# A two-layer hybrid attention block: maxima in steps of two banks, values in fewer and longer visits, and two gate tiles computed earlier

## The chip, the core and the metric

The program runs on one core of a Trainium2 chip. The metric is device time in microseconds, from launch to end. The engines are TensorE (PE, with its weight loads as PEld), VectorE (DVE), ScalarE (ACT), GpSimd (POOL) and SyncE (SP), which here issues DMAs alone. Matmul results land in PSUM, in banks of 512 fp32 columns.

## The reference

A two-layer block for 1024 latent tokens and 256 context tokens of width 1024. In each layer every token is normalised and modulated, projected to 2816 columns, mixed by three groups of heads, multiplied by a SiLU gate, and projected back with a residual. The change touches the first group, attention of all latent tokens to all 1280 tokens:

```python
shift, scale, gate = jnp.split(silu(c) @ w_mod[l] + b_mod[l], 3, axis=-1)
h = rms_norm(x, norm_gain[l]) * (1 + scale[:, None]) + shift[:, None]
aq, ak, av, ag, bz, bg, nq, nk, nv, ng = jnp.split(h @ w_in[l], SPLIT_POINTS, axis=-1)
...
kk = jnp.concatenate([k, k_ctx], axis=1)
vv = jnp.concatenate([v, v_ctx], axis=1)
s = jnp.einsum("bqkgd,bskd->bkgqs", q, k).astype(jnp.float32)
p = jax.nn.softmax(s, axis=-1)
o = jnp.einsum("bkgqs,bskd->bqkgd", p, v)
...
y = jnp.concatenate([a_out * silu(ag), b_out * silu(bg), n_out * silu(ng)], axis=-1) @ w_out[l]
x = x + gate[:, None] * y
```

There are eight query heads of 64 columns in two groups, each with its own key and value head.

## The kernel before, in words

**Stages.** Per layer: the modulation vector and the normalised, modulated, transposed activations, each split in a high and a low part (`hh`, `hl`); the input projections, as three matmuls for a product (high × high, low × high, high × low); neighbourhood attention (and, in layer 0, the context tokens' attention) in 28 units in layer 0 and 16 in layer 1; global attention in eight units; the output projection. In layer 0 the modulation runs in a loop over eight blocks of weights, `mod_rows`, `mod_set` and `first_h`, and the four features of `W` (the pooling projection) for the first 512 tokens are multiplied in the same loop, three blocks behind. The gate products of the attention heads, `gate_feat`, come late in the projection stage: four feature tiles by two halves of the tokens, of 24 matmuls each, stored to DRAM as `agd`.

**A unit of global attention** (`ga_unit`) is a pair of heads and 512 queries. Scores are computed with keys on the partitions, so that the maximum of a query lies across partitions. The maxima are therefore computed apart, with queries on the partitions, from the high parts only: `shift`, twenty steps for a unit, each a 512-column matmul into a single bank (or two of 256 columns), and a DVE reduction. `shift_rows` takes the result through a transpose into an extra row of the second query operand, so that `scores` come out with the maximum subtracted. Scores go by fifths of the keys (`kp` 0 to 4), two heads each: two key tiles into a pair of banks, one exponential of 1024 columns on ACT (L1032), and a running sum over keys on POOL (L1037, L1040), at `kp` 4 on DVE (L1040) with a fold (L1042). `values` multiplies the exponentials by the values into the bank `ps_c` (L1049). `finish` sums over partitions with a matmul by ones (L1058), takes the reciprocal through Ln and Exp on ACT (L1062, L1063) with a Newton step on DVE (L1065, L1066), multiplies by gate and output (POOL L1067, DVE L1068), and `store_u` writes high and low part (ACT L815, DVE L816).

**PSUM.** Three single banks `ps_b` are handed out in turn by `ps_one`, for maxima among others; `ps_c` is the accumulator; four banks `ps_w` serve as single banks in projections and as two pairs in attention, for scores.

**What sets the order.** PE's order is the order of the program text. The other engines' order is set by a scheduler that goes by dependencies, and a tile that is handed out again waits for its readers. Each engine works through its instructions in order, so one that waits holds all behind it. The steps of maxima form one list, `shifts`, of all eight units. `shift_step(n)` takes the next n. Some are taken during neighbourhood attention (`n_ahead`, 29 single-bank steps), and in global attention they are laid between scores and values, four or five for each `kp`. Within one `kp` the order is: scores of head 0, a step, values of the `kp` before for both heads, a step (two at `kp` 4), scores of head 1, two steps. `finish` of the unit before stands at the end of `kp` 2. `early(k, fn)` runs a load at neighbourhood unit k: the keys `gk(0)` and the first queries `gunits[i][4]`.

Of the kernel before, what the change touches and what calls it, by code (L numbers as in the profile page):

```python
# [31 lines left out]
GA_AHEAD = 8  # L32
# [42 lines left out]
def hybrid_block_kernel(  # L75
# [48 lines left out]

    def ps_one(name):
        wide.b += 1
        return ps_b[wide.b % 3]
# [177 lines left out]
    x0 = load_x(0, 4, [rows3(pm.tile([P, D], F32, name="xt", bufs=8)) for _ in range(4)])  # L305
# [25 lines left out]
    def mod_set(j, m):  # L331
        ps = ps_one("ps_sel")
# [7 lines left out]
    blocks = [mod_load(0)]  # L340
    ps = ps_one("ps_v")
# [32 lines left out]
    for l in range(DEPTH):  # L374
# [66 lines left out]


# [65 lines left out]
        else:  # L508
            W = []

            banks = [ps_bank("ps_feat") for _ in range(4)]
            rows = None
            x1 = [rows3(pm.tile([P, D], F32, name="xt", bufs=8)) for _ in range(4)]
            for j in range(KT + 4):
                if j < KT:
                    W.append(load_w_tile([(C_BZ, 512)], j))
                    if j + 1 < KT:
                        blocks.append(mod_load(j + 1))
                    if 2 <= j < 6:
                        load_x(2 + j, 1, x1[j - 2:j - 1])  # L520
                    nxt = mod_rows(blocks[j])
# [3 lines left out]
                if j == 4:  # L525
                    add1, done1 = h_norm(4)
                if 4 <= j < 8:
                    add1(x1[j - 4])
                if j == 7:
                    todo += h_steps(0, 4, done1(), wp, "sig")  # L530
                if j == KT:
# [5 lines left out]
                if j > KT:  # L537
                    fill(2)
                if 3 <= j < KT + 3:
                    for f in range(4):  # L540
                        feat_step(banks[f], W, j - 3, f, 0, 512)
            stx.close()
# [18 lines left out]
        fill(2)  # L561
        for f in range(2, 4):
            pool_in(f, 0, 512, banks[f])
        for t0, n in chunks[1:2]:
# [162 lines left out]
        def gate_out(ps, f, t0, n, s=None):  # L727
            g = s or wp.tile([P, 512], F32, name="gate", bufs=2)
            silu_to(g, ps, 512, s)
            SP.dma_start(out=agd[f, :, t0:t0 + n], in_=g)  # L730

# [4 lines left out]
        gates += [lambda f=f, t0=t0, n=n: gate_feat(f, t0, n) for f in range(4) for t0, n in chunks[:2]]  # L736
# [174 lines left out]
        for pr in range(2):  # L911
# [13 lines left out]
            else:  # L925
                early(s0 + 4, lambda: gk(0))
# [48 lines left out]
        def ga_unit(cc, g, pr):  # L975
# [16 lines left out]
            def shift(i):  # L992

                hi, j = divmod(i, 10)
                if i == 0:
                    load2()
                    st.mx = small.tile([P, 2, 4, 3], F32, tag="gmx", name="gmx")
                q1, mx = st.q1[hi], st.mx[:, hi]
                k1 = gk(g)[0]
                S = ps_one("ps_m")  # L1000
                if j < 8:
                    qt, half = divmod(j, 2)
                    PE.matmul(S, q1[:, qt * P:(qt + 1) * P], k1[:, half * 512:(half + 1) * 512], start=True, stop=True)  # L1003
                    DVE.reduce_max(out=mx[:, qt, half:half + 1], in_=S, axis=AX.X)  # L1004
                    return
                q0 = 2 * (j - 8)
                for i in range(2):
                    PE.matmul(S[:, i * 256:(i + 1) * 256], q1[:, (q0 + i) * P:(q0 + i + 1) * P], k1[:, SEQ:NT], start=True, stop=True)
                DVE.reduce_max(out=mx[:, q0:q0 + 2, 2], in_=S.rearrange("p (a b) -> p a b", a=2), axis=AX.X)
                if hi and j == 9:  # L1010
                    st.nn = small.tile([P, 8], F32, tag="gnn", name="gnn")
                    DVE.tensor_reduce(out=st.nn, in_=st.mx.rearrange("p h q k -> p (h q) k"), op=ALU.max, axis=AX.X, negate=True)
# [11 lines left out]
            def scores(hi, kp):  # L1024
                k1, k2 = gk(g)
                S = ps_pair("ps_st").rearrange("p (a b) -> p a b", a=2)
                for i in range(2):
                    kc = slice((2 * kp + i) * P, (2 * kp + i + 1) * P)
                    PE.matmul(S[:, i, :], k1[:, kc], st.q1[hi], start=True, stop=False)  # L1029
# [306 lines left out]
```

## Time and profile before

| | us |
|---|---|
| median of three runs | 1539.0 |
| the runs | 1536.47 to 1542.13 |
| profiled execution, its own time | 1539.72 |
| its span, first to last instruction | 1537.9 |
| PE busy | 1474.2 |
| DVE busy | 860.2 |
| ACT busy | 637.6 |
| POOL busy | 513.1 |
| layer 0: modulation | 0 to 65 |
| layer 0: neighbourhood and context attention | 391 to 513.3 |
| layer 0: global attention | 513.3 to 730.3 |
| layer 1: neighbourhood attention | 1126.8 to 1226.8 |
| layer 1: global attention | 1226.8 to 1442 |

A row of the timeline gives start, length, engine, line, and, in brackets, how long the engine stood idle before it and what released it. A group gives busy time, mean length of one instruction in ns, and the idle time before them. Line numbers are those of the kernel before. Matmuls overlap, so the time of one is read from start to start. In the orders shown below, lines are those of the kernel that is named.

### The profile page before, as it was taken

Reading aid. Unit: us, or ns where it says so; the run is one execution under the profiler, and the core shown is the slowest. Engines: PE = TensorE matmul, PEld = TensorE weight load, DVE = VectorE, ACT = ScalarE, POOL = GpSimd, SP = SyncE. Lnnn points to the kernel's source line nnn. Section 1 sums busy time; section 2 is a strip of 40 time slices with the busy share of each in tenths; the row PEclk is TensorE's granted clock in tenths of the full one; section 3 lists DMA queues with packets and bytes.
Section 4 is the critical chain, followed back from the end, with each engine's and each line's share of the span. In section 5 each row is a group of like instructions: output and inputs, shape, how many; then the busy total and the mean of one; then the engine's idle time right before and its main releaser. Section 6 shows DMA issues by size and latency. Waiting matters only on the chain.

```text
span 1537.9 us, 22259 instructions
## 1 busy us (share of the span) xinstructions
PE 1474.2 (96%) x8001; PEld 1072.8 (70%) x8001; DVE 860.2 (56%) x1666; ACT 637.6 (41%) x1220; POOL 513.1 (33%) x630
## 2 busy tenths in 40 slices
PE   5999999999999999998999999999998999999999
PEld 3787777788888555553788888878787854544577
DVE  3645234552678678875533543464358868786522
ACT  4543132333676444444312452332466544444400
POOL 0232336000134556565001233460013265565300
PEclk9999999999999999999999999999999999999999
DMA  9436455537745200101413222243697301001331
GB/s 317 140 97 219 133 158 162 165 107 192 178 113 159 73 27 25 39 8 55 168 58 109 76 93 91 85 142 82 155 227 172 89 21 42 21 24 39 133 121 55
DMA packets 153039, 167.91 MB, mean 109 GB/s; under 512 B 35384, under 2 KB 112032, under 8 KB 152864
## 3 DMA queue, kind: packets, MB, share of 16 engines
q1 hardware_dynamic: 152928, 166.48, 37.0%
q8 instruction: 63, 1.03, 0.3%
q14 instruction: 48, 0.39, 0.1%
HBM read 126.45 MB, written 40.86 MB: 109 GB/s over the span
## 4 chain that ended last, share of the span: by engine, by line
PE 80%; DVE 8%; ACT 4%; DMA 3%; issue 3%; SPq 1%; POOL 0%; DVEq 0%; POOLq 0%; ACTq 0%
PE ps_w L418 8%; PE ps_w L419 8%; PE ps_w L420 8%; PE ps_c L1049 8%; PE ps_w L1204 4%; PE ps_w L1207 4%; PE ps_w L1205 4%; PE ps_w L1029 4%; PE ps_b L1003 4%; PE ps_w L1030 3%; PE ps_c L894 3%; PE ps_b L882 2%; PE ps_w L426 2%; PE ps_w L428 2%; PE ps_w L427 2%
## 5 line engine op out<-in xcount | busy, mean ns | idle before, releaser
L1032 ACT ACTIVATE gp<-ps_w 128x1024 f32<-128x1024 f32 x160 | 162.4, 1022 | 190.9 <-PE ps_w L1030 155.3
L418 PE MATMUL ps_w<-wh,hh 128*128 128x512 f32 (+1 forms) x624 | 235.7, 378 | 2.2 <-ACT wh L287 2.2
L419 PE MATMUL ps_w<-wl,hh 128*128 128x512 f32 (+1 forms) x624 | 229.0, 367 | 1.0 <-DVE wl L288 1.0
L420 PE MATMUL ps_w<-wh,hl 128*128 128x512 f32 (+1 forms) x624 | 228.4, 366 | 0.0
L1004 DVE TENSOR_REDUCE gmx<-ps_b 128x1 f32<-128x512 f32 x256 | 171.7, 685 | 73.2 <-PE ps_b L1003 69.0
L1049 PE MATMUL ps_c<-gp,av 128*64 128x512 f32 x640 | 165.0, 609 | 10.3 <-ACT gp L1032 10.3
L1040 POOL TENSOR_TENSOR gacc<-gacc,gp 128x1024 f32<-128x1024 f32 x64 | 161.4, 2548 | 25.8 <-ACT gp L1032 25.5
L418 PEld LDWEIGHTS ps_w<-wh,hh 128*128 128x128 f32 x624 | 118.4, 190 | 27.8 <-issue 4.0
L419 PEld LDWEIGHTS ps_w<-wl,hh 128*128 128x128 f32 x624 | 117.8, 189 | 21.3 <-DVE wl L288 2.2
L420 PEld LDWEIGHTS ps_w<-wh,hl 128*128 128x128 f32 x624 | 117.6, 188 | 21.3
L1030 PE MATMUL ps_w<-gq,kst 128*128 128x512 f32 x320 | 126.7, 396 | 0.0
L1204 PE MATMUL ps_w<-woh,hh 128*128 128x512 f32 x272 | 109.5, 403 | 0.0
L1205 PE MATMUL ps_w<-wol,hh 128*128 128x512 f32 x272 | 107.4, 395 | 0.0
L639 DVE TENSOR_REDUCE qss<-sq 128x8 f32<-128x512 f32 (+2 forms) x58 | 31.1, 537 | 135.7 <-ACT sq L637 135.7
L1049 PEld LDWEIGHTS ps_c<-gp,av 128*64 128x64 f32 x640 | 42.5, 136 | 87.3 <-issue 65.2
L1037 POOL TENSOR_TENSOR gacc<-gp 128x1024 f32<-128x1024 f32 x32 | 75.8, 2369 | 50.0 <-ACT gp L1032 50.0
L288 DVE TENSOR_TENSOR wl<-wraw,wh 128x512 fp32r<-128x512 f32 (+1 forms) x96 | 66.3, 707 | 38.8 <-ACT wh L287 37.4
L1207 PE MATMUL ps_w<-woh,hl 128*128 128x512 f32 x272 | 85.6, 395 | 0.0
L426 PE MATMUL ps_w<-hh,wh 128*128 128x512 f32 (+1 forms) x208 | 81.6, 392 | 2.4 <-ACT wh L287 2.4
L866 ACT ACTIVATE prob<-ps_w,m 128x768 f32<-128x768 f32 (+2 forms) x88 | 72.7, 826 | 19.4 <-DVE m L853 7.4
L428 PE MATMUL ps_w<-hh,wl 128*128 128x512 f32 (+1 forms) x208 | 79.6, 382 | 0.0
L427 PE MATMUL ps_w<-hl,wh 128*128 128x512 f32 (+1 forms) x208 | 79.2, 381 | 0.0
(225 smaller groups left out, 2916.2 us busy)
## 6 DMA issues: line engine op xcount, KB each, us to landing
wmod<-in_w_mod_dram SPq DMA_DIRECT2D x48, 512.0 KB
wraw<-in_w_in_dram SPq DMA_DIRECT2D x64, 256.0 KB
gq<-qad SPq DMA_DIRECT2D x64, 128.0 KB
woraw<-in_w_out_dram SPq DMA_DIRECT2D x14, 512.0 KB
wraw<-in_w_in_dram SPq DMA_DIRECT2D x48, 128.0 KB
kst<-knd SPq DMA_DIRECT2D x16, 320.0 KB
qad<-qkhi SPq DMA_DIRECT2D x18, 256.0 KB
qad<-qklo SPq DMA_DIRECT2D x18, 256.0 KB
```

The source lines that it names most:

```text
L418: PE.matmul(ps[:, :n], a, wh[:, off:off + n], start=(k == 0), stop=False)
L419: PE.matmul(ps[:, :n], a, wl[:, off:off + n], start=False, stop=False)
L420: PE.matmul(ps[:, :n], b, wh[:, off:off + n], start=False, stop=(k == KT - 1))
L426: PE.matmul(ps[:, :n], wh[:, fs], hh[:, k, ts_], start=(k == 0), stop=False)
L1004: DVE.reduce_max(out=mx[:, qt, half:half + 1], in_=S, axis=AX.X)
L1030: PE.matmul(S[:, i, :], k2[:, kc], st.q2[hi], start=False, stop=True)
L1032: ACT.activation(out=p, in_=S, func=AF.Exp)
L1040: eng.tensor_tensor(out=st.acc[hi], in0=st.acc[hi], in1=pf, op=ALU.add)
L1049: PE.matmul(st.o[hi * 64:(hi + 1) * 64, :], av[:, kt, g * 64:(g + 1) * 64], st.p[hi, kp][:, i, :], start=(kt == 0), stop=(kt == NTT - 1))
L1204: PE.matmul(ps[:, i2, :], a, oh[:, cs], start=(k == 0), stop=False)
L1205: PE.matmul(ps[:, i2, :], a, ol[:, cs], start=False, stop=False)
L1207: PE.matmul(ps[:, i2, :], b, oh[:, i2 * 512:(i2 + 1) * 512], start=False, stop=(k == KT - 1))
```

## The change

**Maxima.** Steps of the first unit and of the first head of the second stay as they were. All others are made by `shift2`: five steps a head, each in a pair of banks, with one reduction of 1024 columns; the fifth holds the context keys of all four query tiles. The list has 103 steps instead of 168. 31 of them are taken in neighbourhood attention, one after each of a unit's two heads, in the last 16 units, and the loads of first keys and queries move with them.

**Scores** go to single banks, with one exponential of 512 columns for each. **Values** are taken at `kp` 2 and `kp` 4 for two fifths at a time; the last fifth of a unit comes at `kp` 1 of the next, with its sums and `finish`. `sums` copies them out of PSUM on ACT. In `finish` POOL takes both products with the gate, ACT the high part from POOL's result, DVE the low part. Running sums have buffers of their own (`accs`).

**Gates.** In layer 0, two of the four feature tiles for the first 512 tokens are multiplied in the modulation loop, into two of the `ps_b` banks, with eight loads of 128 KB added; they leave the later gate stage. Vector loads come ahead of the first tokens, and each later token tile is read one block later.

```diff
-GA_AHEAD = 8
+GA_AHEAD = 31
...
+                    G.append((hh[:, j, 512:768], hh[:, j, 768:1024]))
+                    raw = wp.tile([P, 512], F32, name="wraw", bufs=4)
+                    SP.dma_start(out=raw[:, 0:256], in_=w_in[l, j * P:(j + 1) * P, C_AG:C_AG + 256])
+                    split_w(G[j], raw[:, 0:256], slice(0, 256))
...
+                    for f in range(2):
+                        feat_step(ps_b[1 + f], G, j - 3, f, 0, 512)
...
-        gates += [lambda f=f, t0=t0, n=n: gate_feat(f, t0, n) for f in range(4) for t0, n in chunks[:2]]
+        gates += [lambda f=f, t0=t0, n=n: gate_feat(f, t0, n) for f in range(4) for t0, n in chunks[:2]
+                  if l or f > 1 or t0]
...
+            def shift2(hi, j):
+                if j == 0:
+                    (load2 if hi else shift_new)()
+                S = ps_pair("ps_m")
+                if j < 4:
+                    for half in range(2):
+                        shift_mm(hi, S, j, half * 512, half * 512, 512)
+                    DVE.reduce_max(out=st.mx[:, hi, j, 0:1], in_=S, axis=AX.X)
+                    return
+                for qt in range(4):
+                    shift_mm(hi, S, qt, qt * 256, SEQ, 256)
+                DVE.reduce_max(out=st.mx[:, hi, :, 1], in_=S.rearrange("p (a b) -> p a b", a=4), axis=AX.X)
+                shift_head(hi, 2)
...
-                S = ps_pair("ps_st").rearrange("p (a b) -> p a b", a=2)
+                p = ap_.tile([P, 2, 512], F32, name="gp", tag="prob", bufs=PB)
                 for i in range(2):
+                    S = ps_one("ps_st")
...
+                    ACT.activation(out=p[:, i, :], in_=S, func=AF.Exp)
...
+            def sums():
+                S = ps_one("ps_gs")
+                for hi in range(2):
+                    PE.matmul(S[hi * 64:(hi + 1) * 64, :], ones, st.acc[hi][:, 0:512], start=True, stop=True)
+                st.r0, st.t1 = [ap_.tile([P, 512], F32, name=nm, tag="fin", bufs=4) for nm in ("gr0", "gt1")]
+                ACT.activation(out=st.r0, in_=S, func=AF.Ln)
+                ACT.activation(out=st.t1, in_=S, func=AF.Copy)
...
                 POOL.tensor_tensor(out=gt, in0=gt, in1=st.osb, op=ALU.mult)
-                DVE.scalar_tensor_tensor(out=t1, in0=t1, scalar=-1.0, in1=gt, op0=ALU.mult, op1=ALU.mult)
-                store_u(f, cc * 512, 512, t1)
+                POOL.tensor_tensor(out=gt, in0=gt, in1=t1, op=ALU.mult)
+                hi, lo = hh[:, f, cs], hl[:, f, cs]
+                ACT.activation(out=hi, in_=gt, func=AF.Identity, scale=-1.0)
+                DVE.scalar_tensor_tensor(out=lo, in0=gt, scalar=-1.0, in1=hi.bitcast(F32), op0=ALU.mult, op1=ALU.subtract)
...
+        n_shifts = min(len(units), (GA_AHEAD + 1) // 2)
         for i in range(2):
-            early(len(units) - 12, gunits[i][4])
+            early(len(units) - n_shifts - 1, gunits[i][4])
+        early(len(units) - n_shifts, lambda: gk(0))
...
-                if lagv:
-                    lagv(0)
-                    lagv(1)
-                shift_step(2 if kp == 4 else 1)
+                if kp == 1 and pv:
+                    pv[2](4, 0)
+                    pv[2](4, 1)
+                    pv[7]()
+                    pv[3]()
+                elif kp in (2, 4):
+                    for j in range(4):
+                        values(kp - 2 + j // 2, j % 2)
                 scores(1, kp)
-                shift_step(2)
-                if kp == 2 and pv:
-                    pv[3]()
+                shift_step(2 if kp == 0 else 1)
```

ACT, in a middle unit of global attention of the kernel before, around the tail of the previous unit: `gr` is the reciprocal, `hh` the high part of the output, `gp` the exponentials.

```order
L1062 ACTIVATE gr_6166<-ps_b_71 128x512
L1063 ACTIVATE gr_6166<-gr_6166 128x512
L1032 ACTIVATE gp<-ps_w_3845 128x1024
L1032 ACTIVATE gp<-ps_w_3846 128x1024
L815 ACTIVATE hh<-gt_6169 128x512
L1019 ACTIVATE gmr<-ps_b_71 8x128
```

The same place of the changed kernel, with the copy of the values (`gosb`) and of the sums (`gt`) ahead:

```order
L1093 ACTIVATE gosb<-ps_c 128x512
L1100 ACTIVATE gr_5990<-ps_b_70 128x512
L1101 ACTIVATE gt_5991<-ps_b_70 128x512
L1107 ACTIVATE gr_5990<-gr_5990 128x512
L1072 ACTIVATE gp<-ps_b_71 128x512
L1072 ACTIVATE gp<-ps_b_69 128x512
L1072 ACTIVATE gp<-ps_b_70 128x512
L1072 ACTIVATE gp<-ps_b_71 128x512
L1114 ACTIVATE hh<-ggate 128x512
L1072 ACTIVATE gp<-ps_b_69 128x512
L1072 ACTIVATE gp<-ps_b_70 128x512
```

`hh` now reads `ggate`, POOL's product, and stands ahead of the exponentials of head 1 at `kp` 2.

POOL of the changed kernel over one unit (L1077 is the first add of each head, L1080 the others, L1110 and L1112 the two products with the gate):

```order
L1077 TENSOR_TENSOR gacc<-gp 128x1024 x2
L1110 TENSOR_TENSOR ggate<-ggate,gosb 128x512
L1080 TENSOR_TENSOR gacc<-gacc,gp 128x1024
L1112 TENSOR_TENSOR ggate<-ggate,gt_5991 128x512
L1080 TENSOR_TENSOR gacc<-gacc,gp 128x1024 x3
```

In the kernel before there was one product, L1067, behind all six adds; now there are two among them.

SP at the start of neighbourhood attention in layer 1, in the kernel before: `qad` and `kad` hold queries and keys of global attention, `knd` keys of neighbourhood attention.

```order
L372 DMA hh<-qad 64x512 x2
L730 DMA agd<-gate 128x512
L372 DMA hl<-qad 64x512
L793 DMA hh<-knd 64x1280 x2
L834 DMA ngate<-ngd 128x128 x2
```

and in the changed kernel:

```order
L374 DMA hh<-qad 64x512 x2
L447 DMA agd<-gate 128x512
L374 DMA hl<-qad 64x512 x2
L374 DMA hh<-qad 64x512 x2
L374 DMA hl<-qad 64x512 x2
L774 DMA kst<-kad 64x1280 x2
L780 DMA kst<-kad 64x1280
L853 DMA ngate<-ngd 128x128
```

All queries of the first two units and the first keys now stand there together, ahead of the loads for the next neighbourhood units.

More of the change, by code (lines that the diff above doesn't have):

```diff
@@ L123, in hybrid_block_kernel @@
     ps_pair = ps_bank = ps_wide
+    wide.ring = ps_b
     def ps_one(name):
         wide.b += 1
-        return ps_b[wide.b % 3]
+        return wide.ring[wide.b % len(wide.ring)]
     def ps_acc(name):
@@ L340, in hybrid_block_kernel @@
     blocks = [mod_load(0)]
+    x0 = load_x(0, 4, [rows3(pm.tile([P, D], F32, name="xt", bufs=8)) for _ in range(4)])
     ps = ps_one("ps_v")
@@ L511, in hybrid_block_kernel @@
             banks = [ps_bank("ps_feat") for _ in range(4)]
+            wide.ring = ps_b[:1]
+            G = []
             rows = None
@@ L560, in hybrid_block_kernel @@
             pool_in(f, 0, 512, banks[f])
-        fill(2)
+        fill()
         for f in range(2, 4):
             pool_in(f, 0, 512, banks[f])
+        if not l:
+            for f in range(2):
+                gate_out(ps_b[1 + f], f, 0, 512)
+            wide.ring = ps_b
+        fill()
         for t0, n in chunks[1:2]:
@@ L1002, in shift @@
                     qt, half = divmod(j, 2)
-                    PE.matmul(S, q1[:, qt * P:(qt + 1) * P], k1[:, half * 512:(half + 1) * 512], start=True, stop=True)
-                    DVE.reduce_max(out=mx[:, qt, half:half + 1], in_=S, axis=AX.X)
+                    shift_mm(hi, S, qt, 0, half * 512, 512)
+                    DVE.reduce_max(out=st.mx[:, hi, qt, half:half + 1], in_=S, axis=AX.X)
                     return
@@ L1075, in hybrid_block_kernel @@
+            return shift, scores, values, finish, load, shift_rows, shift2, sums
+        gunits = [ga_unit(4 * cc + 2 * g + pr, cc, g, pr) for cc in range(2) for g in range(2) for pr in range(2)]
         shifts = []
         for i, u in enumerate(gunits):
-            own = [lambda u=u, j=j: u[0](j) for j in range(20)]
+            own = []
+            for hi in range(2):
+                way, k = (0, 10) if i + hi < 2 and i < 2 else (6, 5)
+                own += [lambda u=u, way=way, hi=hi, j=j: u[way](hi, j) for j in range(k)]
@@ L1136, in hybrid_block_kernel @@
         nu = len(gunits)
+        nvf = nv.rearrange("p t c -> p (t c)")
+        accs = [[nvf[:, 0:1024], nvf[:, 1024:2048]],
+                [ak_.tile([P, NT], F32, name="gacc", tag="kst", bufs=6)[:, 0:1024] for _ in range(2)]]
         for i in range(nu):
-            _, scores, values, finish, _, _ = gunits[i]
+            _, scores, values, finish = gunits[i][:4]
             pv = gunits[i - 1] if i else None
```

100 lines of the change are left out of this document (43 added, 57 removed).

## The prediction

> **What bounds the kernel now.** I read the windows by stage first, then the groups of the first global attention, then single units in the timeline. The columns of a window are its length and the busy time of PE, PEld, DVE, ACT, POOL, then granted clock, DMA share and GB/s.
>
> ```profile
> core 0: us, PE busy (x) PEld busy (x) DVE busy (x) ACT busy (x) POOL busy (x), PEclk, DMA share, GB/s
> 16.00:65.00 49.00, 48.42 (x312) 34.33 (x312) 23.54 (x62) 23.72 (x47) 8.30 (x12) 1.00 0.82 272
> ...
> 391.00:513.30 122.30, 116.86 (x1099) 100.28 (x1097) 94.88 (x260) 85.81 (x202) 42.80 (x129) 1.00 0.59 156
> 513.30:730.30 217.00, 205.36 (x841) 106.81 (x840) 156.12 (x200) 98.68 (x116) 128.85 (x59) 0.99 0.10 30
> 1126.80:1226.80 100.00, 92.89 (x890) 81.92 (x891) 77.96 (x198) 63.83 (x128) 28.21 (x77) 1.00 0.64 156
> 1226.80:1442.00 215.20, 203.74 (x836) 106.47 (x836) 156.26 (x201) 98.11 (x115) 128.30 (x57) 0.99 0.10 31
> ```
>
> PE fills the projections. In the two global attentions it stands still 11.6 and 11.5 us; there lie DVE at 72% and POOL at 59%. What a steady unit loses is seen at its start:
>
> ```profile
> 617.14 0.50 PE L1003 MATMUL ps_b<-kst,hh 128*128 128x512 f32 x1 [1.24 <-DVE gmx L1004]
> 617.48 0.40 PE L1029 MATMUL ps_w<-hh,kst 128*128 128x512 f32 x1
> 617.71 0.40 PE L1030 MATMUL ps_w<-gq,kst 128*128 128x512 f32 x1
> ...
> 618.41 0.44 PE L1008 MATMUL ps_b<-kst,hh 128*128 128x256 f32 x2
> 618.78 1.94 PE L1049 MATMUL ps_c<-gp,av 128*64 128x512 f32 x8
> 620.64 0.50 PE L1008 MATMUL ps_b<-kst,hh 128*128 128x256 f32 x2
> ```
>
> ```profile
> 644.28 0.50 PE L1003 MATMUL ps_b<-kst,hh 128*128 128x512 f32 x1 [1.25 <-DVE gmx L1004]
> ...
> 644.61 0.40 PE L1029 MATMUL ps_w<-hh,kst 128*128 128x512 f32 x1
> ```
>
> One unit takes 644.61 − 617.48 = 27.13, of which 1.25 is PE waiting for a maxima reduction behind DVE's add. A 512-column matmul takes 0.23 start to start; the eight value rows of one fifth (both heads) 1.86 with their neighbours. The two 256-column steps around them take 0.37 and 0.34 where their width would take 0.23: each change of kind, scores to values and back, costs about 0.35 in all (0.25 by these two steps alone; an estimate).
>
> The last unit is the worst:
>
> ```profile
> 698.41 0.39 PE L1029 MATMUL ps_w<-hh,kst 128*128 128x512 f32 x1
> ...
> 719.80 0.63 ACT L815 ACTIVATE hh<-gt 128x512 fp32r<-128x512 f32 x1 [5.15 <-DVE gt L1068]
> 720.33 1.92 ACT L1032 ACTIVATE gp<-ps_w 128x1024 f32<-128x1024 f32 x2
> ...
> 721.39 1.96 PE L1049 MATMUL ps_c<-gp,av 128*64 128x512 f32 x5 [3.08 <-ACT gp L1032]
> ...
> 730.27 0.50 PE L1204 MATMUL ps_w<-woh,hh 128*128 128x512 f32 x1
> ```
>
> It runs 31.9 us. Its pattern matters for the change: ACT, in order, holds `hh` for a late DVE product, two exponentials queue behind, and PE stops 3.08 us.
>
> **The change, part by part.** Prices in global attention come from these groups (mean ns behind the busy time):
>
> ```profile
> L1032 ACT ACTIVATE gp<-ps_w 128x1024 f32<-128x1024 f32 x80 | 81.2, 1022 | 93.5 <-PE ps_w L1030 75.7 <-POOL gacc L1037 17.7
> L1040 POOL TENSOR_TENSOR gacc<-gacc,gp 128x1024 f32<-128x1024 f32 x32 | 80.7, 2548 | 12.9 <-ACT gp L1032 12.7
> L1004 DVE TENSOR_REDUCE gmx<-ps_b 128x1 f32<-128x512 f32 x104 | 69.7, 686 | 35.8 <-PE ps_b L1003 33.8
> ...
> L1037 POOL TENSOR_TENSOR gacc<-gp 128x1024 f32<-128x1024 f32 x16 | 37.9, 2367 | 24.5 <-ACT gp L1032 24.5
> ...
> L1040 DVE TENSOR_TENSOR gacc<-gacc,gp 128x1024 f32<-128x1024 f32 x16 | 23.1, 1445 | 4.3 <-ACT gp L1032 4.3
> ...
> L1068 DVE SCALAR_TENSOR_TENSOR gt<-gt,ggate 128x512 f32<-128x512 f32 x7 | 16.0, 2286 | 0.2
> ...
> L1042 DVE TENSOR_TENSOR gacc<-gacc 128x512 f32<-128x512 f32 x16 | 10.9, 681 | 0.1
> ...
> L1067 POOL TENSOR_TENSOR ggate<-ggate,gosb 128x512 f32<-128x512 f32 x8 | 10.3, 1291 | 50.3 <-ACT gosb L1053 43.6 <-DVE gmx L1009 6.6
> ...
> L1053 ACT ACTIVATE gosb<-ps_c 128x512 f32<-128x512 f32 x8 | 4.8, 599 | 9.5 <-PE ps_c L1049 7.5 <-PE ps_b L1058 2.0
> ...
> L815 ACT ACTIVATE hh<-gt 128x512 fp32r<-128x512 f32 x7 | 4.4, 630 | 13.3 <-DVE gt L1068 13.3
> ```
>
> ```profile
> L850 DVE TENSOR_REDUCE m<-ps_w 128x1 f32<-128x256 f32 x56 | 23.6, 421 | 13.7 <-PE ps_w L847 12.9
> ```
>
> *Maxima.* No row shows a 1024-wide reduction. 256 more columns cost 0.686 − 0.421 = 0.265, so 0.686 + 2 × 0.265 = 1.22 (between 0.69 and twice it, 1.37). A head then costs DVE 5 × 1.22 = 6.1 instead of 10 × 0.686 = 6.9: 1.6 us less of DVE a unit. PE's columns are the same. That alone does not end a wait: one reduction now holds its bank pair for 1.22, where single banks turned over in 0.69.
>
> *Values.* Five visits a unit become three: one of a fifth, two of two fifths. Two out-and-backs of about 0.35 go; the sums now sit beside the values, a third. PE: −1.05 a unit (bounds −0.75 and −1.2). With the old stall gone as well a unit would be 27.13 − 1.25 − 1.05 = 24.8.
>
> *The tail of the previous unit*, now at kp 1. Count from a unit's first score. PE: 2 score pairs, maxima and the values of one fifth reach 6.7, sums 7.55, scores of head 1, kp 1 end 8.5. ACT then has gosb, Ln, Copy, Exp at 0.6 each, from 7.2 to about 9.5, and only then those two exponentials, to 10.1–10.6. POOL's order is: head 1's first add, gate × values, head 0's add of kp 2, gate × reciprocal. That is 2.37 + 1.29 + 2.55 + 1.29 = 7.5, done at 17.6–18.1. (The product with the reciprocal was DVE's; `L1068`.) ACT's `hh` stands ahead of the exponentials of head 1, kp 2, so these begin at 18.2–18.7 and free their first bank at 18.8–19.3. PE has meanwhile done two fifths of values, those scores and a maxima step, and at 16.0 wants that bank for the second half of the next scores (three banks in the ring). **It stands 2.5 to 3.3 us; I take 2.7.** What bounds this below: were POOL idle when kp 2's first exponentials end, its add and product (3.84) and `hh` would still take about as long as PE's 5.0 us of other work, and the stall would be 0.3. It is not idle, by its order. DVE's low part (`hl`) waits on `hh` too and holds the maxima behind it; PE's next need of these comes some 5 us later, so that is hidden.
>
> *The start of a unit.* DVE takes the last reduction (1.22), the add of head 1's kp 4 (1.2, up to 2.5 beside POOL), this unit's first reduction (1.22). PE wants the second pair back at 2.8, it comes at about 4.4: stall 1.6. The next, behind the fold (0.68), costs 0 to 0.4. So the old 1.25 comes back as 1.6. Single-bank exponentials cost ACT 0.5 to 0.6 for 512 columns against 0.96 (the two of 1.92) for 1024: 0 to 0.3 on PE.
>
> A middle unit: 24.8 + 2.7 + 1.6 + 0.1 = 29.2, which is **+2.1**; five of them **+10.5**.
>
> *The other units.* Unit 0 ran
>
> ```profile
> 513.26 0.51 PE L1029 MATMUL ps_w<-hh,kst 128*128 128x512 f32 x1
> ...
> 536.09 0.40 PE L1029 MATMUL ps_w<-hh,kst 128*128 128x512 f32 x1
> ```
>
> 22.8 us and has no tail before it: −1.1 from fewer visits. Unit 6, with half its maxima gone in both kernels: +0.4. Unit 7 has none; its PE work is ten score pairs of 0.92, six fifths of values of 1.72, two sums of 0.85 and four visits of 0.35, 22.6, and the `hh` stall 2.5: 25.1 for 31.9, **−6.8**. Per layer 10.5 − 1.1 + 0.4 − 6.8 = +3.0, both **+6**.
>
> *Clock.* After the 3.08 us above, one stretch ran at half clock:
>
> ```profile
> 722.30:725.80 3.50, 3.50 (x8) 1.38 (x5) 3.25 (x2) 0.00 (x0) 1.53 (x1) 0.51 0.00 0
> ```
>
> which costs 3.5 × 0.49 = 1.7 us. The 1.25 us waits had none. A 2.7 us stall lies between; by one in five of the twelve stalls I add **+4** (bounds 0 and 20). The Trainium skill, "TensorE: Matmul & The Clock Gate", section "HAM oscillation — how this bites in real kernels", warns of PE gaps over about 3.4 us. By that rule these stalls would drop no clock at all, and the sum would be 4 lower; the trace has the drop after 3.08 us, so the row decides.
>
> *Neighbourhood attention.* 31 steps ahead instead of 29, so less remains: in it lie 2 more steps, about +0.7 of maxima and 0.25–0.35 for each extra visit. In layer 1 the query and key loads now go ahead of the first unit, and the first two maxima stand right behind the last gate product:
>
> ```profile
> 1127.67 1.19 SPq L372 DMA_DIRECT2D hh<-qad  x2
> ...
> DMA packets 13338, 13.24 MB, mean 221 GB/s; under 512 B 8192, under 2 KB 9716, under 8 KB 13332
> ```
>
> ```profile
> 1133.57 0.40 PE L428 MATMUL ps_c<-hh,wl 128*128 128x512 f32 x1
> 1167.87 0.33 PE L882 MATMUL ps_b<-ident,rg 128*128 128x128 f32 x1 [2.62 <-POOL rg L869]
> ```
>
> (The DMA line is that of 1100 to 1160 us.) Eight query loads of 128 KB and two of 320 KB are 1.66 MB, 7.5 us at 221 GB/s, with landing time 1137–1138; PE is there at 1133.8. PE waits about 4, with everything of the first units behind it, and loses 1.7 to the clock; thinner maxima (two a unit, not three) give back about 2 of the waits at DVE and POOL, and visits cost 1.7. **+5** (0 to +8). Layer 0 starts its loads two units early, hidden by the context units' work: **+0.5** (−2 to +2.5).
>
> *Gate products beside the modulation.* 48 matmuls of 0.23 = 11.1 us move from a stage where PE is full into 16–65, where PE is full too (48.42 of 49): even. The 8 loads, 1 MB, at 272 GB/s are 3.9 us of a DMA share of 0.82: covered, unless they come ahead of a modulation block. The vector loads now go ahead of x. I take **−0.7** (−3 to +3.5).
>
> Sum: 1539.7 (the profiled execution) + 6 + 4 + 5 + 0.5 − 0.7 = 1554.5; that execution was 0.7 above the median, so **1554**, its own range 1547 to 1574.
>
> **The rivals.**
> (a) *Faster, bound by PE.* POOL's products come in time and DVE's shorter queue ends the waits: 21.7 + 6 × 24.8 + 22.6 = 193 a layer where 217.0 and 215.2 stood, −46 in both, and with +5 for the rest about 1498. For it: DVE loses the last gate product (2.29 a unit, `L1068`) and over 1 us of maxima. Against it: the product goes to POOL, behind the adds above; only a shorter add could mend that and the mean of 32 is 2.55.
> (b) *Half the stalls.* The `hh` stall is near its low bound, 0.3–1.0, as ACT's exponentials run together and the first add starts 2 us sooner: units about 27.1, so unit 7 wins: −8 a layer; 1539 − 16 + 6 = about 1527.
> (c) *Even.* Stalls of 1.5–2, no clock: 1533–1546.
> (d) *Slower still, through the clock*: it decides from the point where a 2.7 us stall starts half speed each time. Twelve × 1.7 = 20 instead of 4: about 1571–1580. For it the half-speed row; against it, no wait of 1.25 had it.
>
> **How the numbers follow.** Forecast (1547–1570) 0.47; (c) 0.19; (b) 0.12; (a) 0.12; (d) 0.10. This kernel's measurement tells 0.5%, 7.7 us, from no change. Faster than 1531.3: (a), (b) and a little of (c): 0.26. Within: most of (c) and the low end of the forecast: 0.17. Slower than 1546.7: 0.57. The range leaves out most of (a) and the top of (d): 1512 to 1576.
>
> **What would show it.** ACT's `hh` row waiting 2–5 us for POOL's second product in units 1 to 6, followed by PE's second score bank waiting on ACT; unit starts 29 us apart; a maxima wait on DVE of 1.6 near a unit's start; the last unit 25 long; PE idle about 4 us on a load before layer 1's first neighbourhood scores. Unit starts 25 apart and POOL's product done before kp 2's values end would make it wrong.

## The result, and the profile after

| | us |
|---|---|
| before, median (1535.69 to 1542.13) | 1537.74 |
| changed, median of four runs (1596.93 to 1600.29) | 1597.63 |
| ratio | 1.0389, 95% interval 1.0362 to 1.0416 |
| changed, span of the profiled execution | 1595.6 |
| predicted | 1554 (1512 to 1576) |

The change made the kernel 60 us slower. The direction was forecast; the size was not, and lies above the range. Stage by stage, from the first matmul of one stage to that of the next (the first row from the start of the span, the last row to the last matmul):

| stage | before | after | difference | predicted |
|---|---|---|---|---|
| layer 0 up to neighbourhood attention | 391.9 | 404.0 | +12.0 | −0.7 |
| its neighbourhood and context attention | 121.3 | 120.6 | −0.7 | +0.5 |
| its global attention | 217.0 | 240.6 | +23.6 | +5 |
| output projection, layer 1 projections | 396.5 | 394.3 | −2.2 | 0 |
| layer 1 neighbourhood attention | 100.0 | 103.1 | +3.1 | +5 |
| its global attention | 217.0 | 237.5 | +20.5 | +5 |
| rest | 90.1 | 91.5 | +1.4 | 0 |

(The predicted values for global attention hold half each of the +6 for the units and the +4 for the clock.) The windows of the changed kernel, over its two global attentions and two short stretches, with the columns as before:

```profile
core 0: us, PE busy (x) PEld busy (x) DVE busy (x) ACT busy (x) POOL busy (x), PEclk, DMA share, GB/s
524.60:765.20 240.60, 212.71 (x837) 113.27 (x835) 158.91 (x134) 106.46 (x203) 132.54 (x64) 0.93 0.09 27
1262.60:1500.10 237.50, 209.65 (x837) 110.22 (x835) 160.45 (x134) 105.79 (x203) 132.39 (x63) 0.94 0.10 29
...
84.40:94.70 10.30, 3.46 (x11) 2.90 (x12) 3.73 (x6) 6.69 (x11) 0.69 (x1) 0.50 0.14 51
599.80:606.70 6.90, 5.79 (x14) 4.28 (x15) 3.05 (x3) 4.62 (x10) 5.28 (x3) 0.51 0.00 1
```

PE stands still 28 us in each attention instead of 12, and its mean clock is 0.93 and 0.94 there, where it was 0.99. Over 240.6 us, 0.06 is some 14 us. In all, 34 us of layer 0's attention and 27 us of layer 1's lie at half clock, where 3.4 us did in each before. One unit shows both, in the timeline of a middle unit, with the wait before each instruction in brackets:

```profile
627.90 2.40 POOL L1080 TENSOR_TENSOR gacc<-gacc,gp 128x1024 f32<-128x1024 f32 x1
627.93 2.91 DVE L1109 SCALAR_TENSOR_TENSOR gt<-gt,gr 128x512 f32<-128x512 f32 x1
...
630.98 1.26 POOL L1112 TENSOR_TENSOR ggate<-ggate,gt 128x512 f32<-128x512 f32 x1 [0.69 <-DVE gt L1109]
632.28 0.63 ACT L1114 ACTIVATE hh<-ggate 128x512 fp32r<-128x512 f32 x1 [7.49 <-POOL ggate L1112]
632.81 2.07 ACT L1072 ACTIVATE gp<-ps_b 128x512 f32<-128x512 f32 x4
...
633.45 0.51 PE L1070 MATMUL ps_b<-hh,kst 128*128 128x512 f32 x1 [3.23 <-ACT gp L1072]
...
634.42 0.80 PE L1070 MATMUL ps_b<-hl,kst 128*128 128x512 f32 x1
```

This is the predicted chain: POOL's add, POOL's product, `hh`, then the exponentials for which PE waits, 3.23 us. (One row differs: POOL's product waited last for DVE's Newton step, 2.91 us beside POOL's add.) The matmul at 634.42 takes 0.80; from 633.96 on the clock is at half. In the groups over layer 0's attention, busy time, mean ns, and idle time before:

```profile
L1047 DVE TENSOR_REDUCE gmx<-ps_w 128x1 f32<-128x1024 f32 x52 | 62.1, 1217 | 24.0 <-PE ps_w L1020 24.0
...
L1070 PE MATMUL ps_b<-hh,kst 128*128 128x512 f32 x80 | 36.4, 454 | 19.2 <-ACT gp L1072 18.4
...
L1108 DVE TENSOR_TENSOR gt<-gt,gr 128x512 f32<-128x512 f32 x7 | 17.7, 2522 | 3.5 <-ACT gr L1107 3.5
...
L1114 ACT ACTIVATE hh<-ggate 128x512 fp32r<-128x512 f32 x7 | 4.4, 629 | 47.1 <-POOL ggate L1112 47.1
...
L1057 PE MATMUL ps_b<-ident,gnn 128*8 128x128 f32 x7 | 2.6, 375 | 2.9 <-DVE gnn L1017 2.9
```

The 1024-column reduction takes 1.217 us (estimated 1.22). ACT stands 47.1 us for POOL's product, 6.7 a unit. PE's 18.4 us behind it is nearly all that it waits for scores. The last row is a wait that the prediction does not have: 2.9 us in unit 6, where the transpose of the last maxima stands directly behind their last reduction, and a DVE product of 2.81 us comes between.

In the first stage, and at layer 1's first neighbourhood unit:

```profile
91.24 1.11 PE L273 MATMUL ps_b<-ident,xt 128*128 128x128 f32 x4 [8.91 <-DVE gate L442]
```

```profile
1172.30 1.19 PE L1020 MATMUL ps_b<-kst,hh 128*128 128x512 f32 x2 [5.73 <-DMA kst<-kad]
```

The first was not predicted at all: PE wants a bank that holds a gate tile, and that tile's SiLU comes last on ACT, behind four of the pooling projection. The 10.24 us at half clock run from 84.4 to 94.7, 3.4 of them behind the wait. The second was predicted at 4.

### The profile page after: what moved, and what is told of

Same layout as the page of the kernel before. It is cut to its first block, busy times and chain, and to the rows that moved or that the text cites. A ratio compares the mean times of both kernels' runs of the same rounds, so it can differ in the third digit from the quotient of the medians.

```text
span 1595.6 us, 22358 instructions
## 1 busy us (share of the span) xinstructions
PE 1486.0 (93%) x8001; PEld 1085.4 (68%) x8001; DVE 874.6 (55%) x1548; ACT 656.2 (41%) x1404; POOL 524.3 (33%) x642
## 4 chain that ended last, share of the span: by engine, by line
PE 79%; DVE 10%; ACT 3%; issue 3%; DMA 2%; POOL 2%; SPq 1%; DVEq 0%; ACTq 0%; POOLq 0%
PE ps_w L420 8%; PE ps_w L421 8%; PE ps_w L422 7%; PE ps_c L1089 6%; PE ps_w L1255 4%; PE ps_w L1257 4%; PE ps_w L1254 4%; PE ps_b L1070 4%; PE ps_c L913 4%; PE ps_b L901 3%; PE ps_b L1071 3%; PE ps_w L428 3%; PE ps_w L429 3%; PE ps_w L430 3%; PE ps_w L1020 3%
## 5 line engine op out<-in xcount | busy, mean ns | idle before, releaser
L1072 ACT ACTIVATE gp<-ps_b 128x512 f32<-128x512 f32 x320 | 171.9, 600 | 136.4 <-PE ps_b L1071 136.0
L1089 PE MATMUL ps_c<-gp,av 128*64 128x512 f32 x640 | 152.9, 615 | 0.0
L1047 DVE TENSOR_REDUCE gmx<-ps_w 128x1 f32<-128x1024 f32 x104 | 124.3, 1217 | 45.5 <-PE ps_w L1020 45.5
L1071 PE MATMUL ps_b<-gq,kst 128*128 128x512 f32 x320 | 135.6, 424 | 0.0
L1070 PE MATMUL ps_b<-hh,kst 128*128 128x512 f32 x160 | 71.3, 446 | 38.5 <-ACT gp L1072 36.8
L885 ACT ACTIVATE prob<-ps_w,m 128x768 f32<-128x768 f32 (+2 forms) x88 | 72.6, 825 | 24.8 <-DVE m L872 12.1
L1080 POOL TENSOR_TENSOR nv<-nv,gp 128x1024 f32<-128x1024 f32 x32 | 76.2, 2404 | 15.0 <-ACT gp L1072 15.0
L660 ACT ACTIVATE sq<-ps_w 128x512 f32<-128x512 f32 (+2 forms) x58 | 27.9, 481 | 122.7 <-PE ps_w L422 122.7
L906 ACT ACTIVATE probt<-ps_b 128x512 f32<-128x512 f32 (+2 forms) x120 | 58.9, 521 | 41.7 <-PE ps_b L901 41.5
L1070 PE MATMUL ps_b<-hl,kst 128*128 128x512 f32 x160 | 75.4, 471 | 0.3 <-ACT gp L1072 0.2
```

What stands on the lines that cost most here:

```text
L1047: DVE.reduce_max(out=st.mx[:, hi, j, 0:1], in_=S, axis=AX.X)
L1070: PE.matmul(S, k1[:, kc], st.q1[hi], start=True, stop=False)
L1071: PE.matmul(S, k2[:, kc], st.q2[hi], start=False, stop=True)
L1072: ACT.activation(out=p[:, i, :], in_=S, func=AF.Exp)
L1080: eng.tensor_tensor(out=st.acc[hi], in0=st.acc[hi], in1=pf, op=ALU.add)
L1089: PE.matmul(st.o[hi * 64:(hi + 1) * 64, :], av[:, kt, g * 64:(g + 1) * 64], st.p[hi, kp][:, i, :], start=(kt == 0), stop=(kt == NTT - 1))
```

## The experiments

**Which part loses.** Each part of the change alone, on the kernel before. The attention part is the changed kernel with these lines, and what belongs to them in the first stage, taken back; the gate part has them, and global attention as before.

```diff
-            wide.ring = ps_b[:1]
...
-                    G.append((hh[:, j, 512:768], hh[:, j, 768:1024]))
...
-                    for f in range(2):
-                        feat_step(ps_b[1 + f], G, j - 3, f, 0, 512)
...
-                  if l or f > 1 or t0]
```

> The kernel before with the global-attention part of the change alone; gate products, vector loads and banks of the first stage stay as before. Theory: the first 404 us lost 12.0 us against the kernel before (the wait of 8.91 us for a bank at 91 us, 10.24 us at half clock behind it, 1.2 us of smaller waits, 2 us at the start), so about 1597.6 - 12 = 1585.5. Rival, the lost time is of the attention parts' loads and only shows early: above 1594.

> The kernel before with the gate products beside the modulation alone. Theory: +12, about 1550. Rival, as the prediction had it, even: 1537 to 1539. If the two parts of the change add up, this and the attention part alone make the whole: 1537.7 + 12 + 48 = 1597.6.

Measured, against 1538.55 for the kernel before: attention alone 1586.1 (ratio 1.0307, 1.0291 to 1.0322), gates alone 1552.9 (1.0084, 1.0062 to 1.0106). So +47.5 and +14.3, with a sum of 61.9 for the whole's 60: the parts add up, and "even" was wrong for the gates. At the start of the run with gates alone (waits, in us: total, times, longest):

```profile
PE ps_c L327 <- DMA wmod<-in_w_mod_dram: 12.6, 2, 7.4
...
PE ps_b L344 <- DMA vrow<-in_b_mod_dram: 4.4, 1, 4.4
```

The vectors came sooner (4.4 instead of 11.0 us in the kernel before), but the first modulation blocks now came later, and PE began its contiguous work some 3 us later.

**The order of the SiLUs.**

```diff
+        if not l:
+            for f in range(2):
+                gate_out(ps_b[1 + f], f, 0, 512)
+            wide.ring = ps_b
         for f in range(2):
             pool_in(f, 0, 512, banks[f])
...
         for f in range(2, 4):
             pool_in(f, 0, 512, banks[f])
-        if not l:
-            for f in range(2):
-                gate_out(ps_b[1 + f], f, 0, 512)
-            wide.ring = ps_b
```

> The kernel before with the gate products beside the modulation (1552.9 us), the SiLU of the two gate tiles ahead of the four of the pooling projection instead of behind. Theory: PE waits 8.9 us for the bank of a gate tile, whose SiLU stands behind four others on ACT (2 us each); ahead of them the wait falls to 2 to 4, with less at half clock: 1543 to 1548. Rival, the wait only moves to the pooling banks: 1551 to 1554.

1548.4 (1.0056, 1.004 to 1.0073), a gain of 4.5, with intervals that overlap. In the timeline:

```profile
85.73 1.04 PE L273 MATMUL ps_b<-ident,xt 128*128 128x128 f32 x4 [4.32 <-DVE gate L442]
```

The wait halved, to just above the expected 2 to 4, and 3.41 us at half clock are left of 10.24. The other 10 us of this part stay lost; beyond the later start, no run tells where.

**Is it `hh`?** The store is split from `finish` and pinned behind head 1 of `kp` 3:

```diff
-                ACT.activation(out=hi, in_=gt, func=AF.Identity, scale=-1.0)
+            def store():
+                tc.keep_in_program_order(ACT.activation(out=hi, in_=st.gt, func=AF.Identity, scale=-1.0))
...
                 shift_step(2 if kp == 0 else 1)
+                if kp == 3 and pv:
+                    pv[8]()
```

> The changed kernel with one instruction moved: the high part of the output (ACT, hh from POOL's product) is pinned behind the exponentials of head 1 at kp 3; every other instruction stays. Theory A, ACT held by hh and then the half clock: in the changed kernel PE stands 3.23 us a unit for it in twelve units and a 3.41 us stretch at half clock follows (1.7 us); both go, about 12 x 4.9 = 59 us, so about 1540 us, units of 26 to 27 us, no 3 us gap on PE. Rival B, the ring of three single banks with 512-column exponentials is itself too short: a stall of 2 to 3 us stays at the same place, waiting for another exponential, and the time stays above 1580. Rival C, DVE is the bound: the gap moves to the maxima, 1560 to 1580.

> Attention part alone, with hh pinned behind head 1 of kp 3. Theory A: about 1585.5 - 59 = 1527, faster than the kernel before. Rival B: about 1570. Rival C: 1548 to 1568.

With both parts 1587.0 (1.0308), with the attention part alone 1566.3 (1.0178, 1.0163 to 1.0193). Of the 59 us, 11 and 20 came back. The 3.2 us wait went, as theory A says, but others took its place: PE waits 1.9 to 2.2 us for maxima in most middle units, and in some a second time, 1.0 to 1.6. In the attention part alone:

```profile
590.14 3.41 DVE L1061 TENSOR_TENSOR nv<-nv,gp 128x1024 f32<-128x1024 f32 x1 [2.25 <-POOL nv L1061]
...
594.74 0.73 PE L1001 MATMUL ps_w<-kst,hl 128*128 128x512 f32 x2 [1.96 <-DVE gmx L1028]
```

```profile
595.80:602.60 6.80, 5.69 (x15) 3.38 (x15) 5.82 (x7) 2.39 (x4) 0.16 (x1) 0.50 0.00 1
```

DVE's add of `kp` 4 waits 2.25 us for POOL, takes 3.41, and the reduction that PE needs stands behind it: theory C's place. PE waits 1.96 us, and half clock follows again. POOL's products, in the middle of its adds, were late for two readers.

**Does the standing cause the half clock?** Twelve matmuls more in the wait:

```diff
+                    if hi == 0 and kp == 3 and i == 1 and n:
+                        X = wide.t[(wide.n + 1) % 2]
+                        for k in range(12):
+                            PE.matmul(X[:, 0:512], k1[:, 0:P], st.q1[hi], start=True, stop=True)
```

> Attention part alone (1586.1 us) with more work: in every unit but a layer's first, 12 further 512-column matmuls (12 x 0.23 = 2.8 us, result unused, into the pair of banks that is free there) stand ahead of the second score matmul pair of head 0, kp 3, where PE stands 3.2 us for ACT's hh. Nothing else is moved. Theory A: the stay itself keeps its length, but PE is not idle, and the stretches at half clock that follow it (3.4 to 6.8 us each, 1.7 to 3.4 us of time) do not come: 12 units x 1.7 to 2.5, less about 2 us in the two last units whose wait is shorter: about 1560 to 1568. Rival: the half clock has another cause (the units' other waits, or a fixed rhythm): 1586 to 1592.

More work, and faster: 1573.6 (1.0223, 1.0192 to 1.0253) for 1586.1.

```profile
512.00:750.00 238.00, 223.76 (x935) 123.18 (x933) 169.03 (x138) 108.29 (x208) 134.61 (x65) 0.99 0.09 29
```

The clock is at 0.99 instead of 0.93, and middle units take 30.4 us instead of 31.2 to 32.8. So the standing causes the half clock. The gain of 12.5 is below the 18 to 26 expected: a middle unit gained 0.8 to 2.4, and the two last units of a layer, of which one has no such wait and the other a shorter one, lost 1.6 to 1.7 together.

**POOL's products behind its adds.**

```diff
+            def products():
+                tc.keep_in_program_order(POOL.tensor_tensor(out=gt, in0=gt, in1=st.osb, op=ALU.mult))
+                tc.keep_in_program_order(POOL.tensor_tensor(out=gt, in0=gt, in1=st.t1, op=ALU.mult))
...
+                if pv and kp == (2 if i == nu - 1 else 3):
+                    pv[9]()
+                if i > 1 and kp == 0:
+                    gunits[i - 2][8]()
```

> Attention part alone (1586.1 us) with POOL's two gate products pinned behind the unit's last add, and hh pinned behind kp 0 of the unit after. With hh alone moved, PE waited 1.96 us for the maxima instead, with DVE's kp 4 add waiting for POOL. Theory D: POOL's two products (2.6 us) among its adds are late for both readers, hh and the kp 4 adds; with the products in the 10 us in which POOL stands at a unit's start, both waits go, 0.85 us a unit stays, no half clock: units about 25.6 us, a layer's attention about 205 instead of 238, about 1514 to 1520 in all. Rival E: DVE's own queue (1.22 reductions, 2.9 us Newton steps beside POOL) is the bound: waits of 1.5 to 2 us for maxima stay, with half clock, 1555 to 1566.

1544.5 (1.0045, 1.0025 to 1.0065): 41.6 us of the 47.5 are back, and the half clock is gone from middle units. Expected were 66 to 72. The timeline gives the rest, and its cause is near theory E's:

```profile
591.79 0.50 PE L1001 MATMUL ps_w<-kst,hl 128*128 128x512 f32 x1 [1.48 <-DVE gmx L1028]
```

```profile
605.89 7.04 POOL L1061 TENSOR_TENSOR gacc<-gacc,gp 128x1024 f32<-128x1024 f32 x3 [1.05 <-ACT gp L1053]
612.88 2.29 POOL L1095 TENSOR_TENSOR ggate<-ggate,gosb 128x512 f32<-128x512 f32 x1
...
610.97 3.04 DVE L1061 TENSOR_TENSOR gacc<-gacc,gp 128x1024 f32<-128x1024 f32 x1
614.05 1.67 DVE L1063 TENSOR_TENSOR gacc<-gacc 128x512 f32<-128x512 f32 x1
615.64 1.21 DVE L1032 TENSOR_REDUCE gmx<-ps_w 128x4 f32<-128x1024 f32 x1
```

The add and the fold lie beside POOL's work and take 3.04 and 1.67 instead of 1.21 and 0.68. The Trainium skill ("SBUF — State Buffer", section "SBUF: two separate sides") says that a DVE instruction with two SBUF inputs and a GpSimd instruction that reads SBUF take a shared port pair by an exclusive lock, so that the later one waits. These lengths agree with that: DVE's add, 1.21 alone, ends 1.1 us after POOL's last add; POOL's product, 1.26 alone, ends 1.2 after DVE's add; and the fold, 0.68 alone, ends 0.6 after that product.

**The folds out of the way.** They are pinned behind the next unit's second step of maxima:

```diff
-                if kp == 4:
-                    DVE.tensor_tensor(out=st.acc[hi][:, 0:512], in0=st.acc[hi][:, 0:512], in1=st.acc[hi][:, 512:1024], op=ALU.add)
+            def fold():
+                for hi in range(2):
+                    a = st.acc[hi]
+                    tc.keep_in_program_order(DVE.tensor_tensor(out=a[:, 0:512], in0=a[:, 0:512], in1=a[:, 512:1024], op=ALU.add))
```

> The kernel with the late tail (1544.5 us; units of 27.45 us of which 1.47 are PE waiting for a maxima reduction) with one thing more: DVE's two folds of the running sums (0.68 alone, 1.67 beside POOL's product) are pinned behind the second reduction of the unit after, ahead of the sums that read them. Theory: the first fold stands between the kp 4 add and the reduction for which PE waits; without it the reduction comes 1.7 us sooner, PE's 1.47 us wait goes or falls under 0.3 in eleven units: units of 26.0 to 26.3, 1528 to 1532 in all, faster than the kernel before. Rival: DVE's total (adds of 3.0 us beside POOL, reductions of 1.2) sets the wait and the folds only move: 1542 to 1545.

1534.4 (0.9977, 0.9963 to 0.9991): 10 of the expected 12 to 16; units of 26.79, PE's wait 1.12:

```profile
617.52 0.73 PE L1001 MATMUL ps_w<-kst,hl 128*128 128x512 f32 x2 [1.12 <-DVE gmx L1028]
```

This is 0.2% faster than the kernel before, less than the 0.5% by which the prediction called a change.

**Layer 1's neighbourhood attention.** First maxima, queries and keys three units later, with five units of three steps:

```diff
-        n_shifts = min(len(units), (GA_AHEAD + 1) // 2)
+        n_shifts = 13 if last else min(len(units), (GA_AHEAD + 1) // 2)
...
-                    shift_step(1, n_least)
+                    shift_step(2 if last and hi and n >= nun - 5 else 1, n_least)
```

> Attention part alone (1586.1 us), with the first maxima of layer 1 begun three neighbourhood units later (and its loads likewise), the last five units taking three steps. Theory: the wait of 5.4 to 5.7 us for queries and keys ahead of the first unit and 6.83 us at half clock behind it (3.4) go, the three-step units cost 1 to 2: 1578 to 1580. Rival, the loads are bound by the DMA queues and the wait only moves: 1585 to 1587.

1584.7 for 1586.1, not told apart and close to the rival's time: PE now waited for the keys three units later.

```profile
1166.66 0.67 PE L1001 MATMUL ps_b<-kst,hh 128*128 128x512 f32 x1 [5.10 <-DMA kst<-kad]
```

The keys had been issued at 1160.02. Issued two units earlier, beside the fold and one step more between the last reduction and its transpose (`shifts += [lambda: None, gunits[-1][5]]`):

> The same with two more: in layer 1 the first maxima begin three neighbourhood units later and their keys and queries are loaded two units ahead of them (in the run with the loads and maxima moved together PE waited 5.1 us for keys issued 1.3 us earlier); and the last transpose of maxima stands one step later in its list (PE waited 2.88 us a layer for it). Expected: 1530 less 5 (wait for the keys, less the dearer units) less 3.4 (half clock behind it) less 2 x 2.9: 1516 to 1520. Rival: the waits only move, 1528 to 1532.

1526.8 (0.9937, 0.9922 to 0.9952), 7.6 us where some 14 to 18 were expected. The 2.88 us waits of the transposes went. PE's 5.4 us only changed its name: now a gate load came late behind the keys.

```profile
1132.37 0.61 POOL L869 TENSOR_SCALAR rg<-ngate,rr 128x64 f32<-128x64 f32 x2 [5.62 <-DMA ngate<-ngd]
```

One unit later still, with keys and queries behind the first gates:

> The fastest version so far (1526.8 us) with layer 1's first maxima one neighbourhood unit later still and keys and queries loaded one unit later, behind the gate values of the first units: in that version PE waited 5.40 us for POOL, which waited 5.6 us for a gate load behind the keys, and 6.83 us at half clock followed. Expected: that wait and the half clock go, 5.4 + 3.4, less 1 to 2 for two more units of three steps: 1519 to 1521. Rival, the DMA queues are full there and some load is late whatever the order: 1525 to 1528.

1525.8 (0.9911, 0.9891 to 0.993) for 1526.8: not told apart. That wait fell from 5.40 to a single one of 2.50, and no half clock is seen there, so the place was right; the profiled span is 3.3 shorter, the medians only 1.0.

**Are fewer visits a gain?** The visits of two fifths split again, in the version that gave 1526.8:

```diff
                 elif kp in (2, 4):
-                    for j in range(4):
-                        values(kp - 2 + j // 2, j % 2)
+                    for j in range(2):
+                        values(kp - 2, j)
                 scores(1, kp)
+                if kp in (2, 4):
+                    for j in range(2):
+                        values(kp - 1, j)
```

> The fastest version so far (1526.8 us) with the two visits of two fifths of values split into four of one fifth, one before and one behind the scores of head 1; with the last fifth that makes five visits a unit, as in the kernel before. Every instruction is there, on PE alone is the order changed. The prediction priced a visit at about 0.35. Theory: two more visits a unit, 16 units, cost 0.35 each: +11, about 1538, which would be the time of the kernel before. Rival: part of it falls into waits that PE has anyway (1.1 us for the maxima near a unit's start, small ones for score banks): +0 to +5.

Neither: 1516.1 (0.9845, 0.9824 to 0.9867), 10.7 us faster, where a loss of 11 or none was expected. Middle units take 26.23 with no wait of PE above 0.7 us, against 26.79 with one of 1.12. DVE's rows at the same place of a unit tell why, first with two fifths, then split (the next unit begins at 612.5 and at 613.9):

```profile
613.80 1.48 DVE L1061 TENSOR_TENSOR gacc<-gacc,gp 128x1024 f32<-128x1024 f32 x1
615.20 0.15 DVE L998 TENSOR_REDUCE gnn<-gmx 128x4 f32<-128x8 f32 x1
615.27 2.34 DVE L1028 TENSOR_REDUCE gmx<-ps_w 128x1 f32<-128x1024 f32 x2
```

```profile
612.24 1.76 DVE L1061 TENSOR_TENSOR gacc<-gacc,gp 128x1024 f32<-128x1024 f32 x1 [0.45 <-ACT gp L1053]
614.04 1.23 DVE L1032 TENSOR_REDUCE gmx<-ps_w 128x4 f32<-128x1024 f32 x1
...
615.43 1.22 DVE L1028 TENSOR_REDUCE gmx<-ps_w 128x1 f32<-128x1024 f32 x1
```

Two fifths of values ahead of the last scores of head 1 delay these by the time of one more fifth, and with them the exponential and DVE's last add (`L1061`). That add then runs 1.3 to 2.8 us into the next unit, and the first reduction of that unit (`L1028`) begins at 2.8. Split, the add is over 0.2 us after the unit begins, and the reduction begins at 1.6. Two more visits do cost PE 0.56 (26.23 against 26.79 − 1.12 = 25.67), 0.28 each, but what their absence had brought was a wait of 1.1.

That opened the question whether the longer visits are the main loss in the change as it stands:

> The attention part alone as it is in the change (1586.1 us), with only the two visits of two fifths split into four of one fifth, half before and half behind the scores of head 1. Theory, the tail (POOL's products, hh) makes the loss and the longer visits only add the wait at a unit's start: PE's work between kp 2's first scores and the bank it wants is the same, so the 3.2 us and the half clock stay; 0.85 us at a unit's start goes, 0.7 for two more visits comes: 1582 to 1588. Rival, the two-fifth visits cause most of the loss: under 1565.

1564.7 (1.0168, 1.0143 to 1.0192): 21.4 faster than the attention part as changed, twice what theory allowed, and at the rival's bound. The `hh` chain still holds PE, but for 2.25 to 2.41 us and in another place:

```profile
612.33 0.63 ACT L1095 ACTIVATE hh<-ggate 128x512 fp32r<-128x512 f32 x1 [4.36 <-POOL ggate L1093]
...
613.49 0.27 PE L1038 MATMUL ps_b<-ident,gnn 128*8 128x128 f32 x1 [2.25 <-ACT gp L1053]
```

Units take 28.8 to 31.4 us for 31.2 to 32.8, and 17 us of layer 0's attention are at half clock instead of 34. So, mended alone, the visits are worth 21.4 us and POOL's products with `hh` 41.6; with the tail mended, the visits are worth 10.7. The other half of what they gave was probably waiting and half clock that the mended tail ends as well; no run separates the two.

**All repairs together**, attention part alone:

> The version with five visits (1516.1 us) and the neighbourhood order of layer 1 in which PE's wait of 5.4 us for POOL fell to 2.5 with no half clock behind it. Between the two versions without five visits that order gave 1.0 by median and 3.3 by the profiled spans. Theory: 5.25 + 3.4 go, 2.5 and dearer units come: 1510 to 1514. Rival: loads only wait elsewhere: 1515 to 1517.

1513.1 (0.9834, 0.9812 to 0.9857), the fastest. Against 1516.1 this is not a clear gain. The neighbourhood wait is 2.59 us in its profile, and here 3.41 us at half clock do follow it. The version keeps of the change the pairs of banks for maxima, the single banks for scores and the last fifth in the next unit, none of which was tried alone; POOL's products stand behind its adds, and the five visits and the gate tiles are as in the kernel before.

```profile
511.60:718.80 207.20, 204.68 (x850) 104.17 (x848) 166.28 (x137) 108.79 (x208) 145.70 (x65) 1.00 0.11 33
1214.60:1422.00 207.40, 204.72 (x850) 104.20 (x848) 166.16 (x137) 108.52 (x208) 145.46 (x63) 1.00 0.11 34
```

These windows run 3 us into the output projection, whose first matmuls stand at 715.47 and 1418.83. So the stage takes 203.9 and 204.2 us, 13 us less than before, with PE standing 2.5 to 2.7 us, at full clock.

## Why the prediction was wrong

*Direction and main mechanism: right.* "It stands 2.5 to 3.3 us; I take 2.7" measured 3.23 in ten units and 2.0 in the last of each layer. The order of POOL, ACT's `hh` and the ring of three banks were named as they came. Moving POOL's products and `hh` out of the way (late tail) gave back 41.6 us. That the length fits is partly luck: in the unit shown, PE stops 18.0 us after the unit's start and POOL's product is done at 20.1, where 16.0 and 17.6 to 18.1 were written. Both came 2 us late, and the product also waited 0.69 us for DVE, which was not in the sum.

*"By one in five of the twelve stalls I add +4" failed; in the attention this is the largest miss.* Half-speed stretches followed eleven of the twelve stalls, all but the one of 1.99 us in layer 1's last unit. With 34 and 27 us at half clock instead of 3.4 each, of which half is lost where PE works, the clock took some 24 to 27 us in the two attentions, where 4 was written with a bound of 20. (A part of it lies behind the wait for the transposes and at the start of layer 0's stage.) A middle unit took 31.7 us on average, where 29.2 was written: PE's work, 25.67 by the version with late folds, and the waits of 3.23 and 0.86 make 29.8, and about 2.0 is left for the half clock. It was rival (d), at 0.10, that came true, and at 1571 to 1580 it too was short, mostly by the next term. That stretch had one precedent in the rows, 3.08 us; a stall of about that length should have been priced as that row says. By the rule cited from the Trainium skill ("TensorE: Matmul & The Clock Gate", section "HAM oscillation — how this bites in real kernels"), gaps over about 3.4 us, there would have been none: here 3.23 and 1.96 us were enough, 1.25 and 1.48 were not. What decides is shown in the last section.

*"Even" for the gate products failed*: +12.0 in the stage, +14.3 alone. The matmuls balance, as said. What the prediction left out is who waits for the two banks that they hold: ring, SiLU order and transposes (8.91 us, and half clock for 3.4 us behind it), and that the modulation loads now come behind the vectors (some 3 us). With the SiLUs in the other order 10 us of it stayed, so the cause of most of this part is open. Its bound of +3.5 was too narrow.

*"−1.05 a unit" for the removed visits was too large, and the term decides something else.* PE's work in a middle unit, without its wait, was 25.88 before (27.13 − 1.25) and is 25.67 in the version with late folds, where 24.8 was written: −0.2. Two visits alone are worth 0.56. What takes the rest back is open; maxima and scores have as many matmuls as before, but from start to start the scores, now in single banks, take 10.2 us of a unit instead of 9.4. And what the longer visits delay, the last scores, was left out: it is worth 10.7 to 21.4 us.

*"Stall 1.6 at the start of a unit"* measured 0.86 beside the `hh` stall, and 1.5 to 2.0 where that was mended: here one wait hid the next.

*Layer 1's keys, "PE waits about 4"* measured 5.73; the stage +3.1 for +5. *The last unit, "25.1 for 31.9"*: the two last units of a layer together took 57.5 and 57.0 us; they were 58.6 before and are 52.2 by the prediction's terms. Of the 5 us between, 2.9 are PE's wait for the transposes, with half clock behind it. The version with late folds still has it and takes 58.7 and 59.6 for the two units; with one more step in its place (1526.8 us) they take 53.0 and 54.9.

*Rival (a)*, bound by PE at 1498, was never reached: the best version has 204 us an attention where it had 193.

## What to carry to other kernels

When work is moved on one engine, follow each reader of each result in the new place, and the engine's other readers too: here two products among POOL's adds were late for two engines at once, and a longer visit on PE delayed an add on DVE by way of ACT. A pause on PE costs more than its length as soon as the rows show half clock after pauses of that size. Price each repetition of such a pause that way, and not one in five. Mend one wait and read the trace again: here one wait hid the next four times.

## What the runs showed of the hardware that was not expected

- The stretches at half clock lie on fixed steps of 3.413 us. In layer 0's attention of the changed kernel they begin at 524.74, 569.11, 599.83, 633.96, 664.68, 695.40, 722.71 and 753.43 us, which are 13, 9, 10, 9, 9, 8 and 9 such steps apart, and each lasts one step or two (3.41 or 6.83 us).
- What counts is how long PE stands within one such step. From 400 to 1500 us, the profiles of all sixteen kernels, each with its own first step, have 4982 steps at full clock. Half clock followed each of the 86 in which PE stood 1.93 us or more, none of those in which it stood less than 1.1 us, and 22 of the 115 between. So one length of pause can go either way. The 2.19 us ahead of the last sums of the 1526.8 us version brought half clock in layer 1, where they fell in one step, and none in layer 0, where 1.77 us fell in one and the rest in another. By this count, as an estimate for pauses that may begin anywhere in a step, one of 2.7 us is followed by half clock about two times in three or more, and one of 3.23 us at least four times in five. What decides between 1.1 and 1.93 us is open; the profile's ends of matmuls are modelled, which blurs it.
- Filling the pause with unused matmuls ended the half clock in the middle units and made the kernel 12.5 us faster.
- DVE's products of 128×512 take 2.5 us on average beside POOL's adds (17.7 us for seven), where the fold of the same size takes 0.69.
